# The opening of a two-layer block on one core: more warming products, sums of squares on another engine, and a product moved

## The chip, the cores and the metric

The kernel runs on one core of a Trainium2 chip. The metric is device time in microseconds (us), from one launch. A core has TensorE (PE in the profile; PEld is its weight loading), VectorE (DVE), ScalarE (ACT), GpSimd (POOL) and SyncE (SP), which here only issues transfers. Each works through its own instructions in order; semaphores tie them together.

## The reference, cut to what matters

A two-layer block and a third mixing block are applied to 256 tokens of width 1024, in float32. Only the start of the first layer is touched by the change:

```
h  = rmsnorm(x, a_norm_attn)                # x * rsqrt(mean(x*x) + eps) * gain
z  = h @ a_w_in                             # q, k (768 each), v (768), qm (256)
q, k = rope(q), rope(k)
o_self = diff_attention(q, k, v)            # 6 heads of 2 x 64
kv = rmsnorm(mem, a_mem_norm) @ a_w_mem_kv  # memory keys, values (256 each)
o_mem  = softmax(qm @ mk / 8) @ mv          # 4 heads
x  = x + concat(o_self, o_mem) @ a_w_out
```

After it come an MLP, a second layer of the same kind with its MLP, and the mixing block with a gated MLP.

## The kernel before, in words

Activations lie transposed, 8 chunks of 128 features by 256 tokens. To keep float32 accuracy each operand is split: `hi` is a rounded copy (written by ScalarE, L206, L191, L270, L276), `lo` is the rest (VectorE, L216, L192, L271, L280), and a product is three matmuls, hi x hi, hi x lo and lo x hi.

The product work is a list of **units**. A unit is one weight tile (512 KB) and 24 matmuls of 256 columns. In the opening: units 0 to 5 are the values `v` (three `tok_block`s, PSUM name `tp`), units 6 and 7 the memory queries `qm` (`fp`), units 8 to 11 the memory keys and values from `hMa` (two of `fp`, two of `tp`), units 12 and 13 the first query-key block (`fp`), and so on through six query-key blocks. Norms are applied late: the products use x times the gain, and the row factor rsqrt(mean) comes in when PSUM is read. So the sum of squares `ssq_A` is needed by two small products, `mst` (L374's input, per token) and `ms` (L348's input, per column), whose results become `rstdt_A`, `rstd_A` and then the scaled rope tables `ropeR` (L905, POOL).

`Stat.add` (L302 to L308) forms that sum: ScalarE squares a chunk into `sq` (four buffers), and an addition onto `acc` follows, seven for eight chunks, on POOL.

The order of all else is set by a planner at build time. `Order.t` is a model clock that advances with the matmuls alone, 106.7 ns for one of 256 columns (a float32 one of 256 columns counts 427 ns). Side jobs are generators: `yield 450` means to go on at the first poll after 450 ns of model time, and polls come between matmuls, after 4, 10, 12, 16, 22 and 24 of a `tok_block` unit and after each 4 of a `feat_block` unit. At a poll, due side jobs are written first and then at most one piece of weight preparation (`hi` of a tile, then the two halves of `lo`) for a tile about 2.25 to 4 units ahead. So each engine has a fixed order, and a position in it can be given as the number of matmuls issued before it ("position 88"). In the first layer a weight transfer is issued by SP when a tile's second `lo` half is done (four `raw` buffers).

`first_inputs` (from L929) issues the first transfers, puts 10 warming products of `ones` on TensorE (L939), which write a tile nobody reads, and splits the first chunks. `squares()` starts the eight additions with 450 ns between them and then `tok_stat` and `row_stat` with a delay of 3500. `memory_a()` splits the memory into `hMa` chunk by chunk (hi, 600, lo, 500) and sums its squares (`ssq_M`) from model time 9200. `lambdas()` puts small operations on VectorE from 15000 (identb, maskb, lscr). `mem_pair` is the attention of two memory heads; the first is spawned after the first query-key block and the second after the second. `head_a` is the attention of one self head, spawned 6500 after its query-key block; it begins with the scores `S`, which need `q` and `k` from the rope (VectorE L623, L624, then POOL L625, L626).

PSUM tiles `acc` have four buffers, taken in turn: each block takes the two that the block before last has given back.

Of the kernel before, what the change touches and what calls it, by code (L numbers as in the profile page):

```python
# [13 lines left out]
OP = mybir.AluOpType  # L14
# [94 lines left out]
def block_kernel(ctx: ExitStack, tc: tile.TileContext, a, out):  # L109
    nc = tc.nc  # L110
# [10 lines left out]
    O = Order()  # L121
    E = SimpleNamespace()
# [10 lines left out]
    def ps_tile(name):  # L133
        return psB.tile([P, 512], F32, tag="ps", name=name)

    def w_tile(name, shape=(P, S), bufs=2):
        return phase[1].tile(list(shape), F32, tag=name, name=name, bufs=bufs)
# [4 lines left out]
    def s_tile(name, n, bufs=4):  # L142
        return small.tile([P, n], F32, tag=name, name=name, bufs=bufs)
# [26 lines left out]
    def hook(fn):  # L170
        plan.append((len(wlist), 0, fn))
# [117 lines left out]


    class Stat:
        def __init__(self, name):
            self.acc = big.tile([P, S], F32, tag="ssq", name="ssq_" + name, bufs=2)
            self.first = None
            self.n = 0

        def add(self, src, keep=False):
            if keep:
                sq = w_tile("sqk", bufs=KC)
            else:  # L300
                sq = wk.tile([P, S], F32, tag="sq", name="sq", bufs=4)
            nc.scalar.activation(sq, src, AF.Square)  # L302
            if self.n == 0:
                self.first = sq
            elif self.n == 1:
                nc.gpsimd.tensor_tensor(self.acc, self.first, sq, OP.add)
            else:
                nc.gpsimd.tensor_tensor(self.acc, self.acc, sq, OP.add)  # L308
            self.n += 1
            return sq  # L310

# [40 lines left out]
    def rstd_tile(name):  # L352
        return big.tile([P, S], F32, tag="rstd", name="rstd_" + name, bufs=3)

    def row_stat(st, name, then=None, delay=1000, tile_fn=None, table=None):
        yield delay
        yield from O.take("rs")
        y = rstd_tile(name)
        v, src = yield from ms_row(st.acc, D, tile_fn=tile_fn)
        yield from rsqrt_(y, v, then=table, src=src)  # L360
        O.give("rs")
        setattr(E, "r" + name, y)
        if then:
            then()
        O.mark("r" + name)

    def tok_stat(st, name, delay=1000):
        yield delay
        yield from O.take("ps")
        p = ps_tile("mst")  # L370
        for j in range(2):
            mm(p[:, 2 * j:2 * j + 2], st.acc[:, j * P:(j + 1) * P], ones[:, 0:2], start=True, stop=True)
        v = s_tile("msvt", 4)
        nc.vector.tensor_scalar(v, p[:, 0:4], 1.0 / D, EPS, OP.mult, OP.add)  # L374
        y = big.tile([P, 4], F32, tag="rstdt", name="rstdt_" + name, bufs=3)
        yield from rsqrt_(y, v, src=(p[:, 0:4], 1.0 / D, epsc[:, 0:1], 1))
        setattr(E, "t" + name, y)
        O.mark("t" + name)
# [392 lines left out]
    PAUSE_MA = (1500, 0, 1100, 2000, 600, 2200)  # L771
# [65 lines left out]
    def mem_kv(src, h, kv):  # L837
        def evac_k(n, p):
            O.need("rM")
            if n == 0:  # L840
                pool = phase[1] if kv == "ma" else big
                setattr(E, kv + "k", pool.tile([P, 2, S], F32, tag="mk", name=kv + "k", bufs=1))
                setattr(E, kv + "v", pool.tile([P, 2, S], F32, tag="mv", name=kv + "v", bufs=1))
            nc.vector.tensor_tensor(getattr(E, kv + "k")[:, n, :], p, E.rM, OP.mult)
            if n == 1:
                O.mark(kv + "k")
        feat_block(src[0], lambda: (h(), h()), evac_k)
        put_v = scaled_tok(lambda: getattr(E, kv + "v"), 0, "tM")

        def evac_v(j, p):  # L850
            put_v(j, p)
            if j == 1:
                O.mark(kv + "v")
        tok_block(src[1], 256, h, evac_v)
# [73 lines left out]
    def first_inputs():  # L928
        nc.scalar.dma_start(par[:, 0:C_LAM], a["par"][:, 0:C_LAM])  # L929
        for i in range(4):  # L930
            nc.sync.dma_start(xT[:, 2 * i:2 * i + 2, :], a["xT"][:, 2 * i:2 * i + 2, :])
            w_load((slice(2 * (i % 2), 2 * (i % 2) + 2),), i % 2)
        w_load()
        w_load()
        E.hA = operand("hA")
        stA = Stat("A")
        warm = ps_tile("warm")
        for _ in range(10):
            nc.tensor.matmul(warm[:, 0:P], ones, ones, start=True, stop=True)  # L939
        for k in range(KC):  # L940
            split_scaled(E.hA, k, xT[:, k, :], gain(G_A_ATTN, k))
            if k % 2:
                w_split(k // 4, slice(k % 4 - 1, k % 4 + 1))
        w_piece()
        w_piece()
        w_piece()

        def tables():
            E.tr = rope_tables(E.rope_a, E.rA)

        def squares():
            for k in range(KC):
                stA.add(xT[:, k, :])
                yield 450
            O.spawn(tok_stat(stA, "A", 3500))
            O.spawn(row_stat(stA, "A", tables, 3500))

        def second_inputs():
            nc.sync.dma_start(memT, a["memT"])
            yield 8100  # L960
            nc.sync.dma_start(E.rope_a, a["rope_a"])
            nc.sync.dma_start(par[:, C_LAM:C_END], a["par"][:, C_LAM:C_END])
            nc.sync.dma_start(cst, a["cst"])

        O.spawn(squares())
        O.spawn(second_inputs())
        E.v = p_tile("vA", (P, 2, 768))
        E.o = operand("oA")
        O.spawn(lambdas(), 15000)
        O.spawn(bias_rows(), 40000)  # L970
        O.spawn(memory_a(), 9200)
        O.spawn(memory_b())

    def lambdas():
# [24 lines left out]
    def memory_a():  # L999
        E.hMa = operand("hMa")  # L1000
        stM = Stat("M")
        yield from split_chunks(E.hMa, memT, G_A_MEM, 500, stM)
        O.spawn(row_stat(stM, "M", None, 3000))
        O.spawn(tok_stat(stM, "M", 3000))
        O.mark("hMa")
# [8 lines left out]
    def wait_for(key, fn):  # L1014
        def get():
            O.need(key)
            return fn()
        return get
# [4 lines left out]
        tok_block(a["w_a_v"][i], 256, lambda: E.hA, scaled_tok(lambda: E.v, 256 * i, "tA"),  # L1023
                  acc_tile if i else ps_tile, "tA")
    mem_queries(a["w_a_qm"], lambda: E.hA, "rA")
    mem_kv(a["w_a_mem"], wait_for("hMa", lambda: E.hMa), "ma")
    for h in range(6):
        qk_block(a["w_a_qk"][h], lambda: (E.hA, E.hA), wait_for("rA", lambda: E.tr),
                 lambda q, k, h=h: head_a(h, q, k), 6500)
        if h in (0, 1):  # L1030
            hook(lambda h=h: O.spawn(mem_pair(h, "ma", 6 + h, "oA", PAUSE_MA)))
    mem_kv(a["w_b_mem"], wait_for("hMb", lambda: E.hMb), "mb")

    def staged(first, stat, g, last, name, also=None):
# [572 lines left out]
```

## Time and profile before

| what | value |
|---|---|
| median of 3 runs | 943.23 us (942.23 to 943.95) |
| profiled execution | 943.52 us, of which the span is 941.7 us |
| busy share | PE 97%, PEld 91%, DVE 73%, ACT 58%, POOL 21% |
| mean granted TensorE clock | 0.993 of full speed |
| share of the chain that ended last | PE 80%, DVE 8%, ACT 5%, POOL 3%, DMA 2% |

The span runs from the first instruction to the last; 1.8 us lie around it. The page also shows the span in 40 slices of 23.5 us; the change lies in the first five. A row of the timeline gives start, duration, engine, line, operation, output and inputs, and in brackets how long the engine was idle before it and who ended that.

### The profile page before, as it was taken

What the parts mean: (1) busy time and instruction counts of PE and PEld (TensorE: products, weight loads), DVE (VectorE), ACT (ScalarE), POOL (GpSimd) and SP (SyncE); (2) the same over time, 40 slices, a digit from 0 to 9 for tenths busy, and PEclk for the clock granted to TensorE, in tenths of its full rate; (3) what the DMA queues carried; (4) which work ended last, traced back from release to release, by engine and by line L of the source; (5) the groups of instructions that cost most, each with busy time, mean ns of one, the idle gap of its engine ahead of it and who ended that gap; (6) DMA issues with size and microseconds to landing.
All of it is one profiled execution on the core that took longest, in us unless ns stands there. A gap on an engine that the chain in (4) does not pass through costs nothing.

```text
span 941.7 us, 17731 instructions
## 1 busy us (share of the span) xinstructions
PE 916.3 (97%) x6768; PEld 855.2 (91%) x6768; DVE 688.9 (73%) x1434; ACT 549.5 (58%) x1063; POOL 199.4 (21%) x238
## 2 busy tenths in 40 slices
PE   7899999999999999999999999999898999999998
PEld 7898899999999998899999999999877989999998
DVE  6979978776666598876776666687956788766664
ACT  6747666665555574656665555566475666545551
POOL 3415633000000042322000000055656421001010
PEclk9899999999999999999999999999999999999999
DMA  8653444565555535333575555574413456665551
GB/s 288 200 178 112 149 145 127 193 229 191 195 185 192 187 119 197 107 118 94 189 255 180 179 187 193 188 259 144 134 67 114 155 172 194 217 200 169 195 199 46
DMA packets 45686, 161.10 MB, mean 171 GB/s; under 512 B 5128, under 2 KB 6800, under 8 KB 45216
## 3 DMA queue, kind: packets, MB, share of 16 engines
q1 hardware_dynamic: 45104, 158.14, 51.3%
q0 software_dynamic: 208, 1.63, 0.6%
q8 instruction: 53, 0.87, 0.4%
q14 instruction: 33, 0.27, 0.1%
q10 hardware_dynamic: 288, 0.18, 0.1%
HBM read 158.88 MB, written 2.63 MB: 172 GB/s over the span
## 4 chain that ended last, share of the span: by engine, by line
PE 80%; DVE 8%; ACT 5%; POOL 3%; DMA 2%; issue 2%; DVEq 0%; SPq 0%; POOLq 0%; ACTq 0%
PE fp L149 40%; PE acc L149 32%; DVE lo L216 2%; PE tp L149 2%; ACT hi L206 2%; PE S L149 1%; DMA raw<-in_w_a_v_dram 1%; POOL rsh L625 1%; PE O L149 1%; PE Sm L149 1%; PE T L154 1%; PE ms L149 1%; DVE xT L603 1%; DVE nm L678 1%; POOL ssq_A L308 1%
## 5 line engine op out<-in xcount | busy, mean ns | idle before, releaser
L216 DVE TENSOR_TENSOR lo<-raw,hi 128x512 fp32r<-128x512 f32 (+1 forms) x555 | 381.5, 733 | 134.9 <-ACT hi L206 134.4
L206 ACT ACTIVATE hi<-raw 128x1024 fp32r<-128x1024 f32 x287 | 296.2, 1053 | 124.9 <-PE acc L149 47.8
L149 PE MATMUL acc<-u,hi 128*128 128x256 f32 x1376 | 245.0, 281 | 0.0
L149 PEld LDWEIGHTS acc<-u,hi 128*128 128x128 f32 x1376 | 210.5, 188 | 0.0
L149 PE MATMUL acc<-u,lo 128*128 128x256 f32 x688 | 193.0, 281 | 0.0
L149 PEld LDWEIGHTS acc<-u,lo 128*128 128x128 f32 x688 | 129.9, 189 | 0.0
L149 PE MATMUL fp<-hW,hi 128*128 128x512 f32 (+1 forms) x368 | 96.2, 384 | 0.1
L450 ACT ACTIVATE uc<-fp 128x256 f32<-128x256 f32 x108 | 39.4, 379 | 63.6 <-PE fp L149 63.6
L149 PE MATMUL fp<-hV,hi 128*128 128x512 f32 (+1 forms) x272 | 70.1, 381 | 0.0
L149 PE MATMUL fp<-hU,hi 128*128 128x512 f32 (+1 forms) x272 | 70.0, 381 | 0.0
L149 PEld LDWEIGHTS fp<-hW,hi 128*128 128x128 f32 x368 | 61.4, 188 | 7.6 <-DVE uc L453 0.3
L453 DVE TENSOR_TENSOR uc<-fp,uc 128x256 f32<-128x256 f32 x108 | 43.8, 418 | 28.5 <-ACT uc L450 27.7
L149 PEld LDWEIGHTS fp<-hW,lo 128*128 128x128 f32 x352 | 53.6, 188 | 7.2
L149 PE MATMUL fp<-hW,lo 128*128 128x256 f32 x352 | 55.9, 281 | 0.0
L149 PEld LDWEIGHTS fp<-hV,hi 128*128 128x128 f32 x272 | 45.2, 189 | 5.2
L149 PEld LDWEIGHTS fp<-hU,hi 128*128 128x128 f32 x272 | 45.2, 188 | 5.2
L875 ACT ACTIVATE uu<-uc 128x256 f32<-128x256 f32 x64 | 24.1, 418 | 39.2 <-DVE uc L871 39.2
L890 POOL TENSOR_TENSOR uc<-uc,rstd_W 128x256 f32<-128x256 f32 x22 | 15.9, 743 | 146.0 <-ACT uc L888 146.0
L149 PE MATMUL fp<-hZ,hi 128*128 128x256 f32 x304 | 45.1, 287 | 0.0
L149 PEld LDWEIGHTS fp<-hV,lo 128*128 128x128 f32 x256 | 38.9, 188 | 5.3
L149 PEld LDWEIGHTS fp<-hU,lo 128*128 128x128 f32 x256 | 38.9, 188 | 5.2
L598 DVE TENSOR_TENSOR u<-uu,u 128x256 fp32r<-128x256 f32 x64 | 24.3, 422 | 25.4 <-ACT u L596 25.4
(345 smaller groups left out, 1634.0 us busy)
## 6 DMA issues: line engine op xcount, KB each, us to landing
raw<-in_w_a_up_dram SPq DMA_DIRECT2D x32, 512.0 KB, 4.7
raw<-in_w_a_down_dram SPq DMA_DIRECT2D x32, 512.0 KB, 4.5
raw<-in_w_b_up_dram SPq DMA_DIRECT2D x32, 512.0 KB, 4.6
raw<-in_w_b_down_dram SPq DMA_DIRECT2D x32, 512.0 KB, 4.7
raw<-in_w_gate_dram SPq DMA_DIRECT2D x22, 512.0 KB, 4.5
raw<-in_w_up_dram SPq DMA_DIRECT2D x22, 512.0 KB, 4.7
raw<-in_w_down_dram SPq DMA_DIRECT2D x22, 512.0 KB, 4.5
raw<-in_w_a_qk_dram SPq DMA_DIRECT2D x12, 512.0 KB, 4.3
```

The lines of the kernel that those rows point to most:

```text
L149: nc.tensor.matmul(dst, lhsT, rhs, **kw)
L154: nc.tensor.transpose(dst, src, ident)
L206: nc.scalar.activation(hi, raw, AF.Copy)
L216: eng.tensor_tensor(lo[sl], raw[sl], f32v(hi[sl]), OP.subtract)
L308: nc.gpsimd.tensor_tensor(self.acc, self.acc, sq, OP.add)
L450: nc.scalar.activation(c, p[:, S:2 * S], AF.Copy)
L453: nc.vector.tensor_tensor(c, p[:, 0:S], c, OP.add)
L598: nc.vector.tensor_tensor(u[:, 1, n, :], us[n], f32v(u[:, 0, n, :]), OP.subtract)
L603: nc.vector.tensor_tensor(x, bank, x, OP.add)
L625: nc.gpsimd.tensor_tensor(sh, sh, sinr, OP.mult)
L875: nc.scalar.activation(u, t, AF.Square)
L890: nc.gpsimd.tensor_tensor(g, g, rs, OP.mult)
```

## The change

Three things, all in the first layer's opening:

1. 15 warming products on TensorE in place of 10.
2. The seven additions of `ssq_A` go to VectorE (`ssq_M` and all later sums stay on POOL). The delay of the two small products behind them is 4500 in place of 3500, and `memory_a()` starts at model time 12000 in place of 9200.
3. The memory product (`mem_kv`, four units) is put behind the first query-key block: units 8 and 9 are now query-key block 0, units 10 to 13 the memory product. The two memory attentions are spawned after query-key blocks 1 and 2 in place of 0 and 1.

```diff
     class Stat:
-        def __init__(self, name):
+        def __init__(self, name, engine=None):
+            self.engine = engine or nc.gpsimd
...
             elif self.n == 1:
-                nc.gpsimd.tensor_tensor(self.acc, self.first, sq, OP.add)
+                self.engine.tensor_tensor(self.acc, self.first, sq, OP.add)
             else:
-                nc.gpsimd.tensor_tensor(self.acc, self.acc, sq, OP.add)
+                self.engine.tensor_tensor(self.acc, self.acc, sq, OP.add)
...
-        stA = Stat("A")
+        stA = Stat("A", nc.vector)
         warm = ps_tile("warm")
-        for _ in range(10):
+        for _ in range(15):
             nc.tensor.matmul(warm[:, 0:P], ones, ones, start=True, stop=True)
...
-            O.spawn(tok_stat(stA, "A", 3500))
-            O.spawn(row_stat(stA, "A", tables, 3500))
+            O.spawn(tok_stat(stA, "A", 4500))
+            O.spawn(row_stat(stA, "A", tables, 4500))
...
-        O.spawn(memory_a(), 9200)
+        O.spawn(memory_a(), 12000)
...
-    mem_kv(a["w_a_mem"], wait_for("hMa", lambda: E.hMa), "ma")
     for h in range(6):
         qk_block(a["w_a_qk"][h], lambda: (E.hA, E.hA), wait_for("rA", lambda: E.tr),
                  lambda q, k, h=h: head_a(h, q, k), 6500)
-        if h in (0, 1):
-            hook(lambda h=h: O.spawn(mem_pair(h, "ma", 6 + h, "oA", PAUSE_MA)))
+        if h == 0:
+            mem_kv(a["w_a_mem"], wait_for("hMa", lambda: E.hMa), "ma")
+        if h in (1, 2):
+            hook(lambda h=h: O.spawn(mem_pair(h - 1, "ma", 5 + h, "oA", PAUSE_MA)))
     mem_kv(a["w_b_mem"], wait_for("hMb", lambda: E.hMb), "mb")
```

## Rows read from the trace of the kernel before

**Rows 1.** The page's busy time of each engine, share of the span, instructions.
```profile
PE 916.3 (97%) x6768; PEld 855.2 (91%) x6768; DVE 688.9 (73%) x1434; ACT 549.5 (58%) x1063; POOL 199.4 (21%) x238
```

**Rows 2.** The waits of PE, whole span: us in total, times, longest.
```profile
PE mst L149 <- POOL ssq_A L308: 2.8, 1, 2.8
PE fp L149 <- DVE hMa L280: 2.7, 2, 2.2
...
PE ms L149 <- ACT osq L751: 2.1, 2, 1.1
```

**Rows 3.** Timeline of PE, units 0 to 4: start, duration, instruction, idle before.
```profile
1.06 3.84 PE L939 MATMUL warm<-ones 128*128 128x128 f32 x20 [1.06 <-DVE ones L254]
7.04 1.02 PE L149 MATMUL tp<-hi,hA 128*128 128x256 f32 x4 [2.15 <-ACT hi L191]
...
11.56 0.64 PE L149 MATMUL tp<-hi,hA 128*128 128x256 f32 x4
...
14.44 0.64 PE L149 MATMUL tp<-hi,hA 128*128 128x256 f32 x4
...
18.70 0.63 PE L149 MATMUL tp<-hi,hA 128*128 128x256 f32 x4
22.11 0.61 PE L149 MATMUL mst<-ones,ssq_A 128*128 128x2 f32 x4 [2.77 <-POOL ssq_A L308]
...
24.04 0.64 PE L149 MATMUL tp<-hi,hA 128*128 128x256 f32 x4
```

**Rows 4.** Timeline of PE, units 8 to 14, memory product and first query-key block.
```profile
35.35 1.11 PE L149 MATMUL fp<-hMa,hi 128*128 128x256 f32 x8
...
42.14 0.58 PE L149 MATMUL fp<-hMa,hi 128*128 128x256 f32 x1 [2.17 <-DVE hMa L280]
...
59.21 1.12 PE L149 MATMUL fp<-hA,hi 128*128 128x256 f32 x8
```

**Rows 5.** Stretches: PE, PEld, DVE, ACT, POOL busy, granted clock, DMA share, GB/s.
```profile
9.00:10.00 1.00, 1.00 (x6) 1.00 (x6) 1.00 (x4) 1.00 (x3) 0.00 (x0) 0.50 1.04 342
...
21.00:22.00 1.00, 0.00 (x0) 0.00 (x0) 1.00 (x2) 0.00 (x0) 1.00 (x1) 1.00 1.01 401
...
46.00:47.00 1.00, 1.00 (x6) 1.00 (x6) 0.96 (x4) 0.87 (x3) 0.00 (x0) 0.50 0.89 283
```

**Rows 6.** Timeline of ACT: the third tile's hi and the last square.
```profile
12.55 1.06 ACT L206 ACTIVATE hi<-raw 128x1024 fp32r<-128x1024 f32 x1 [1.41 <-DMA raw<-in_w_a_v_dram]
...
17.66 0.40 ACT L302 ACTIVATE sq<-xT 128x256 f32<-128x256 f32 x1
```

**Rows 7.** Timeline of DVE: lo halves, statistics, last hMa, first rope.
```profile
15.82 6.78 DVE L216 TENSOR_TENSOR lo<-raw,hi 128x512 fp32r<-128x512 f32 x6 [0.88 <-ACT hi L206]
22.75 0.16 DVE L374 TENSOR_SCALAR msvt<-mst 128x4 f32<-128x4 f32 x1
...
25.71 0.42 DVE L337 TENSOR_TENSOR rs256t<-rs256y 128x256 f32<-128x256 f32 x1
...
41.61 0.47 DVE L280 SCALAR_TENSOR_TENSOR hMa<-memT,par,hMa 128x256 fp32r<-128x256 f32 x1
...
58.48 0.41 DVE L623 TENSOR_TENSOR rt<-fp,ropeR 128x256 f32<-128x256 f32 x1
```

**Rows 8.** Timeline of POOL: sum for x, rope tables, first rope.
```profile
15.61 6.44 POOL L308 TENSOR_TENSOR ssq_A<-ssq_A,sq 128x256 f32<-128x256 f32 x6
...
30.32 3.75 POOL L905 TENSOR_TENSOR ropeR<-rope_a,rstd_A 128x256 f32<-128x256 f32 x4 [2.28 <-DVE hMa L280]
...
61.85 1.05 POOL L626 TENSOR_TENSOR k<-rt,rsh 128x256 f32<-128x256 f32 x1
```

**Rows 9.** DVE by line, 42.1 to 53.6 us, POOL idle: busy, mean ns.
```profile
L216 DVE TENSOR_TENSOR lo<-raw,hi 128x512 fp32r<-128x512 f32 x10 | 6.4, 681 | 1.4 <-ACT hi L206 1.4
```

**Rows 10.** Busy time in longer stretches (columns as in Rows 5).
```profile
22.10:42.10 20.00, 17.34 (x141) 16.88 (x141) 18.34 (x37) 14.95 (x33) 11.19 (x14) 0.98 0.62 204
...
59.20:85.00 25.80, 24.98 (x185) 21.50 (x183) 23.63 (x60) 16.97 (x51) 11.21 (x13) 1.00 0.37 120
```

## The prediction

> **What bounds the kernel now.** I read the page's busy line first: TensorE is busy for 916.3 of 941.7 us [rows 1], so time can come only from stretches where it stands or runs at a low clock. Then PE's waits: of those 25.4 us of idleness 2.8 are for the sum of squares on POOL and 2.7 for the memory's low parts [rows 2], both in the opening. PE's timeline puts them in place. The warming products end at 4.90, PE stands 2.15 us, and unit 0 then takes 4.52 us (7.04 to 11.56) where unit 1 takes 2.88 (11.56 to 14.44) [rows 3]. The stretches tell why: the clock is at 0.50, its 1.2 GHz level, in 9 to 10 us [rows 5]. From 19.33 to 22.11 PE stands for `ssq_A` [rows 3]. In units 8 to 13 it waits twice for low parts of `hMa`, 2.7 us in all [rows 2], the second time for 2.17 [rows 4], and behind that the clock is at 0.50 again, as in 46 to 47 us [rows 5].
>
> The second reading is of DVE. While POOL adds squares, six low halves take 6.78 us, 1.13 each [rows 7]; with POOL idle ten take 6.4, 0.64 each [rows 9]. From 22.1 to 42.1 DVE is busy for 18.34 of 20 us [rows 10]: it runs that stretch, and PE catches up with it at 42.1. That decides the second half of the change.
>
> **The change part by part.** The sum is made against the profiled execution, 943.5 us (941.7 of span and 1.8 around it), 0.3 above the median of the runs.
>
> *Five more warming products.* Twenty records of ten products take 3.84 us, so five more take 1.9 and end at 6.8, still before the first real product at 7.04 [rows 3]. They delay nothing; PE's gap shrinks from 2.15 to about 0.2 us, and unit 0 should run at full clock, 1.6 us shorter. Little of that arrives: unit 2 needs the high part of the third tile, whose transfer ends at 12.55 and whose copy ends at 13.61 [rows 6], against 14.44 now [rows 3]. So the gain is at most 0.83; its first low half then takes 0.64 [rows 9] to about 14.3, 0.2 us after unit 2 would ask for it. Bounds 0 and 0.85; I take 0.7.
>
> *Sums on VectorE.* The trace has no addition of two SBUF tiles of 128x256 on DVE there, but a multiplication of that shape takes 0.42 us and starts 0.45 before its successor [rows 7]. Seven cost 2.9 to 3.2 us (with POOL in the way they could cost 0.9 each, nearer to its own 1.07 [rows 8], but POOL then has nothing to do). Against that, six low halves lose their company: 6 x (1.13 - 0.64) = 2.9 us. DVE is even. In its order four additions stand ahead of the fourth tile's first low half, the last two behind its second half. With squares of 0.40 us as now, the last at 17.66 [rows 6], I get DVE at 14.9, four additions to 16.7, low half to 17.3, addition, low half to 18.3, two additions to 19.2. The sum is ready at 19.2, not 22.06 (POOL's end [rows 8]).
>
> *The delay of 4500.* Today the two small products stand at position 88: PE has issued 14 groups of six and four more when it stops [rows 3]. One thousand model ns are 9.4 matmuls; the next poll puts them at position 96, the end of unit 3. PE gets there at 16.7 + 2.9 = 19.65, after 19.2. The wait of 2.77 goes. Bounds: 2.3 (sum half a microsecond late) and 2.8; I take 2.8. Unit 4 starts at about 20.5 in place of 24.04. SP's queue loses nothing: its weight transfers follow low halves that end at or before today's times, and the rope tables' transfer stands at the same place in its order.
>
> *Memory product behind the first query-key block.* Today 35.35 to 59.21 [rows 4] holds six units and the memory's own statistics: 6 x 2.88 + 0.8 = 18.1 us of 23.9. The excess, 5.8, is 2.7 of waits and 3.1 of half clock. Now the positions. `memory_a` moves from 9200 to 12000, so its last low part from position 188 to 220 (eight chunks, 16 matmuls apart in the later units); its first use, chunk 7 in the second memory unit, moves from 224 to 272. That is 16 matmuls or 1.9 us more slack. But PE comes 3.5 us earlier and DVE does not: it stands at the statistics at about 22.4, after the low halves queued there, against 22.75 now. From there to the last low part of `hMa` it needs today's 19.3 us (22.75 to 42.08 [rows 7]), plus three more low halves (1.9 [rows 9]) and the two `qm` operations (0.7, each like the rope's first [rows 7]), which the new order puts ahead, less some 1.0 of today's 1.66 us of idleness [rows 10]. That is 43.3. PE asks for it at 20.5 + (272 - 96)/24 x 2.88 + 0.8 = 42.4: a wait of 0.9.
>
> What is late next: the values' units (12 and 13) take the PSUM buffers of query-key block 0, which DVE must have read in its rope, placed at position 240 behind three further low halves: it begins at 45.2 and frees the first buffer at 46.0. PE would be at unit 12 at 45.2; 0.8 more. Then head 0's scores, which stand at about position 300 (spawned 6500 after block 0). Behind them on PE everything queues. The rope takes 4.4 us from DVE's first operation to `k` (58.48 to 62.90 [rows 7, 8]), so `k` is ready at about 49.5, and PE reaches the scores at 47.4: 2.1. Together 3.8 us of waits in place of 5.8, each under the length at which the clock fell: gain 2.0. Bounds: nothing gained if DVE is 2 us later than this, and 5.8 if its company with POOL (rope tables 3.75 us [rows 8] and memory sums) costs less than today.
>
> The granted clock kept 1.00 over the wait of 2.77 us, as in 21 to 22 us, and fell to 0.50 over those of 2.15 and 2.17 [rows 3, 4, 5]. The Trainium skill ("TensorE: Matmul & The Clock Gate", What's actually happening) says why one cannot count on either: the activity window runs freely, so the point of change differs from run to run. By that rule the three new waits, too, may cost a fall of 3.1 us in some runs; the trace agrees in that a longer gap was harmless and shorter ones were not.
>
> *Attention spread anew.* Head 0 comes four units earlier and memory pairs 0 and 1 two units later; heads 1 to 5 keep their positions. The largest of today's waits there is 2.1 us in two parts, for head 0's and another head's squares on ACT [rows 2], while DVE is busy 23.6 of 25.8 us from 59.2 to 85.0 [rows 10]. It starts this stretch some 5 us behind PE and has 2.2 of slack in it to catch up, so I add 0.6 us of waits, between the two bounds: -1, if head 0's early start takes half of those waits away, and +3, if the part of the 5 us that the slack doesn't cover is met as waits.
>
> Sum: -0.7 - 2.8 - 2.0 + 0.6 = -4.9, so 943.5 - 4.9 = 938.6. What follows the first layer's output product is untouched, and PE is busy there nearly throughout, so the gain should pass to the end.
>
> **The rivals.**
>
> *DVE does not hold the memory units back.* If low halves beside the rope tables run at 0.64 and the waits of 3.8 us vanish, the gain is 0.7 + 2.8 + 5.8 = 9.3: about 934.5. For it: sums for x no longer hinder DVE. Against: DVE's 18.34 us busy of 20 without slack.
>
> *The clock falls in the new waits.* The second half's gain becomes 2.0 - 3.1 = -1.1 and the total -0.7 - 2.8 + 1.1 + 0.6 = -1.8: 941.7, about the line where no change can be told (0.2% or 1.9 us is what a measurement of this kernel can tell). For it: a gap of 2.1 us stands before the scores. Against: PE works right up to it.
>
> *The sum is late after all.* If squares or additions slip behind the low halves, PE stands for 2 us at position 96 as it did at 88; total -2.9: 940.6.
>
> *Slower: DVE becomes the bound of the opening.* All the low halves between positions 96 and 240 (15) at 1.13 in place of 0.64, with the three or so already counted as slow left out, would put DVE's rope of block 0 some 6 us later. PE then stands 6 us at head 0's scores, the clock falls (3.1), and against the 4.9 gained this gives +4.2: 947.7. It decides from about 5 us of added DVE delay. For it: the first low halves beside POOL did run at 1.13. Against: POOL has only 14 operations in 22 to 42 us [rows 10], and seven fewer before.
>
> **How the numbers follow.** The forecast's own case (936.5 to 940.9) 0.54 with the late sum in it; waits gone (933.5 to 936.5) 0.16; falling clock 0.20 (940.9 to 943.5), half of it within 0.2%; slower 0.06; a change that its own later waits eat up, no difference, 0.04. Faster by over 0.2%: 0.54 + 0.16 + 0.10 = 0.80; within: 0.10 + 0.04 = 0.14; slower: 0.06. The range is 934.2 to 942.4; it leaves out some of the best case and of the worst, 0.2 together.
>
> **What would show it.** Warming ends near 6.8 and the clock stays at 1.00 in 7 to 11 us; unit 2 starts near 13.7. No wait before `mst`; unit 4 near 20.5; low halves at about 0.65 in 16 to 22 us. The first query-key block at about 31.8 without a long wait; waits of PE for `hMa`, for the rope's buffers or for `k` of about 1 to 2 us each between 41 and 50. The prediction is wrong if `mst` still waits over 1 us, if the clock is at 0.50 anywhere in 40 to 55, or if waits in 55 to 120 exceed 6 us.

## The result, and the profile after

The changed kernel takes 947.99 us (median of 5 runs, 946.69 to 948.97). Its time relative to the kernel before is 1.0058, 95% interval 1.0044 to 1.0072: slower by 0.58%, where the prediction named 0.2% as what a measurement of this kernel can tell. The forecast was 938.6, and 947.99 lies outside its range. The profiled execution took 947.97 us, 4.45 more than that of before. Of the 947.97 us 2.3 lie around the span, in place of 1.8.

The page's first lines of after:

```profile
span 945.7 us, 17749 instructions
...
PE 918.9 (97%) x6778; PEld 856.8 (91%) x6778; DVE 686.4 (73%) x1441; ACT 549.4 (58%) x1063; POOL 191.0 (20%) x231
```

Against [rows 1] PE is busy 2.6 us longer for 10 records more, while DVE and POOL are busy for less. PE's timeline of after shows where the time goes (start, duration, instruction, idle before):

```profile
1.05 6.19 PE L940 MATMUL warm<-ones 128*128 128x128 f32 x30 [1.05 <-DVE ones L254]
7.00 0.72 PE L149 MATMUL tp<-hi,hA 128*128 128x256 f32 x4
...
13.50 0.74 PE L149 MATMUL tp<-hi,hA 128*128 128x256 f32 x4 [0.20 <-ACT hi L206]
...
19.80 0.50 PE L149 MATMUL mst<-ones,ssq_A 128*128 128x2 f32 x4
...
20.50 0.82 PE L149 MATMUL tp<-hi,hA 128*128 128x256 f32 x4
...
42.63 1.19 PE L149 MATMUL fp<-hMa,hi 128*128 128x256 f32 x8 [3.36 <-DVE qm L862]
...
57.69 1.12 PE L149 MATMUL fp<-hA,hi 128*128 128x256 f32 x8
...
87.42 0.55 PE L154 MATMUL T<-cst,dw 128*128 128x128 f32 x3 [2.04 <-DVE brow L922]
...
120.86 0.70 PE L149 MATMUL ms<-osq,ones 128*128 128x256 f32 x2 [2.27 <-ACT osq L752]
131.66 0.39 PE L149 MATMUL acc<-oA,hi 128*128 128x256 f32 x2
```

Four marks cut the opening into pieces that can be set against before: unit 4 (20.50, before 24.04), unit 14 (57.69, before 59.21 [rows 4]), the first layer's output product `acc<-oA` (131.66, before 127.49) and the end of the span.

| piece | before | after | difference at equal work | forecast |
|---|---|---|---|---|
| start to unit 4 | 24.04 | 20.50 | -3.5 | -3.5 |
| unit 4 to unit 14 | 35.17 | 37.19 | +0.9 | -2.0 |
| unit 14 to `acc<-oA` | 68.28 | 73.97 | +6.3 | +0.6 |
| `acc<-oA` to the end, and around the span | | | +0.8 | 0 |

("At equal work": head 0's scores, 1.1 us on PE, now lie ahead of unit 14; they are taken from the second piece and added to the third. One pair of `ms` products, 0.5 us, lies ahead of `acc<-oA` in after and behind it in before; it is taken from the third piece and added to the last. The last has 0.45 us around the span in it.)

The clock and the busy time of DVE, in stretches of after (columns as in [rows 5]):

```profile
7.00:11.00 4.00, 4.00 (x36) 3.98 (x35) 3.96 (x9) 3.76 (x9) 0.00 (x0) 1.00 0.99 339
...
26.00:46.00 20.00, 15.71 (x122) 15.13 (x121) 19.40 (x36) 14.75 (x30) 10.91 (x14) 0.95 0.58 205
44.00:47.00 3.00, 3.00 (x15) 2.82 (x14) 3.00 (x8) 1.06 (x1) 0.00 (x0) 0.51 0.67 201
59.20:85.00 25.80, 24.00 (x184) 20.89 (x182) 19.48 (x49) 16.45 (x41) 10.15 (x12) 1.00 0.42 132
88.00:92.00 4.00, 4.00 (x16) 3.25 (x16) 2.55 (x9) 3.83 (x14) 0.71 (x2) 0.57 0.08 17
122.00:126.00 4.00, 4.00 (x24) 3.67 (x24) 2.75 (x9) 1.83 (x3) 2.46 (x4) 0.57 0.38 136
```

The clock now stays at 1.00 in 7 to 11 us. In 26 to 46 DVE is busy for 19.40 of 20 us: it is the engine that runs there, and PE stands. In 59.2 to 85, where before has DVE busy for 23.63 us [rows 10], after has 19.48: DVE has more idle time there, so it isn't short of capacity. Behind the waits at 42.63, 87.42 and 120.86 the clock falls.

PE's waits from 57 to 135 us (total, times, longest), first in before, where the largest of the three stands in [rows 2] (2.1 us; 3.9 in all), then in after:

```profile
PE S L149 <- POOL k L626: 1.0, 1, 1.0
PE OA L149 <- ACT wT L698: 0.8, 1, 0.8
```

```profile
PE ms L149 <- ACT osq L752: 2.3, 1, 2.3
PE T L154 <- DVE brow L922: 2.0, 1, 2.0
PE Tm L154 <- ACT rs256l L320: 1.3, 1, 1.3
PE Tm L154 <- ACT wTm L814: 0.6, 1, 0.6
PE pbias L149 <- DVE on L758: 0.5, 1, 0.5
PE T L154 <- ACT wTm L814: 0.2, 1, 0.2
```

After's six are 6.9 us, 3.0 more than before. The two falls of the clock (88 to 92 and 122 to 126 us, granted 0.57 in each stretch) cost 2 x 4 x 0.43 = 3.4 more. Together that is the piece's 6.3, within 0.1.

DVE's timeline of after, first the sums, then the end of the memory split and the rope, then the place where PE waits for `brow`:

```profile
14.69 0.42 DVE L307 TENSOR_TENSOR ssq_A<-sq 128x256 f32<-128x256 f32 x1
15.21 1.48 DVE L309 TENSOR_TENSOR ssq_A<-ssq_A,sq 128x256 f32<-128x256 f32 x3
...
18.15 0.95 DVE L309 TENSOR_TENSOR ssq_A<-ssq_A,sq 128x256 f32<-128x256 f32 x2
19.02 3.10 DVE L216 TENSOR_TENSOR lo<-raw,hi 128x512 fp32r<-128x512 f32 x5
22.03 0.16 DVE L375 TENSOR_SCALAR msvt<-mst 128x4 f32<-128x4 f32 x1
...
42.07 0.74 DVE L862 SCALAR_TENSOR_TENSOR qm<-fp,rstd_A 128x256 f32<-128x256 f32 x2
...
44.34 0.47 DVE L280 SCALAR_TENSOR_TENSOR hMa<-memT,par,hMa 128x256 fp32r<-128x256 f32 x1
...
46.54 0.41 DVE L624 TENSOR_TENSOR rt<-fp,ropeR 128x256 f32<-128x256 f32 x1
...
84.04 0.48 DVE L758 SCALAR_TENSOR_TENSOR on<-OA,subg,ors 128x256 f32<-128x256 f32 x1 [1.11 <-POOL ors L334]
...
86.83 0.54 DVE L922 COPY brow<-pbias 8x384 f32<-8x384 f32 x1
```

The sums end at about 19.1, low halves without POOL beside them go at 0.62 us (five in 3.10) where [rows 7] has 1.13. But `msvt` begins at 22.03, only 0.7 us earlier than in before, and the last low part of `hMa` ends at 44.81 where before has 42.08 [rows 7] (by the prediction's positions the changed order puts three low halves and `qm` ahead of it). PE gained 3.5 us up to unit 4; DVE gained 0.7.

### The profile page after: what moved, and what is told of

Same layout as the page of the kernel before. It is cut to its first block, busy times and chain, and to the rows that moved or that the text cites. A ratio compares the mean times of both kernels' runs of the same rounds, so it can differ in the third digit from the quotient of the medians.

```text
span 945.7 us, 17749 instructions
## 1 busy us (share of the span) xinstructions
PE 918.9 (97%) x6778; PEld 856.8 (91%) x6778; DVE 686.4 (73%) x1441; ACT 549.4 (58%) x1063; POOL 191.0 (20%) x231
## 4 chain that ended last, share of the span: by engine, by line
PE 78%; DVE 9%; ACT 5%; DMA 3%; issue 3%; POOL 2%; DVEq 0%; SPq 0%; ACTq 0%; POOLq 0%
PE fp L149 39%; PE acc L149 32%; DVE lo L216 3%; ACT hi L206 2%; PE tp L149 2%; PE S L149 1%; DMA raw<-in_w_a_v_dram 1%; POOL rsh L626 1%; PE T L154 1%; PE O L149 1%; DMA raw<-in_w_a_qm_dram 1%; PE ms L149 1%; PE Sm L149 1%; DVE xT L604 1%; DVE hZ L616 1%
## 5 line engine op out<-in xcount | busy, mean ns | idle before, releaser
L216 DVE TENSOR_TENSOR lo<-raw,hi 128x512 fp32r<-128x512 f32 (+1 forms) x555 | 377.2, 726 | 139.9 <-ACT hi L206 139.4
L149 PEld LDWEIGHTS fp<-hW,lo 128*128 128x128 f32 x352 | 53.6, 188 | 7.2
```

Of the source, the lines that this page charges most:

```text
L149: nc.tensor.matmul(dst, lhsT, rhs, **kw)
L216: eng.tensor_tensor(lo[sl], raw[sl], f32v(hi[sl]), OP.subtract)
```

## The experiments

Theory after the first look: the loss comes from the move behind query-key block 0, by what it does to the positions of side jobs in 57 to 130 us. Rival: DVE, which the sums load, is late in the opening, and all the rest follows from that. Ratios are against the kernel before, run beside each kernel; line numbers in the diffs are left out.

### The two halves by themselves

Opening alone, the kernel before with the first two parts, but `memory_a()` still at 9200:

```diff
+        stA = Stat("A", nc.vector)
...
+        for _ in range(15):           # warming
...
+            O.spawn(tok_stat(stA, "A", 4500))
+            O.spawn(row_stat(stA, "A", tables, 4500))
```

> The kernel before with 15 warming products, the sum of squares on VectorE and the delay of 4500; the memory product stays in front of query-key block 0 and the memory split starts at 9200 as before. Theory (the opening is sound, the loss comes from the new order of the memory product): PE reaches unit 4 at about 20.5 us as in the changed kernel, 3.5 us ahead of the kernel before, and the time is 2 to 4 us below the kernel before (939 to 941), because the wait for the memory's low parts may grow by what PE is ahead. Rival (the seven additions put VectorE so far behind that the attention stretch pays for it): no gain or slower, 943 to 948, with waits of over 6 us between 58 and 132 us as in the changed kernel.

Move alone, the kernel before with the third part and `memory_a()` at 12000:

```diff
+        if h == 0:
+            mem_kv(a["w_a_mem"], wait_for("hMa", lambda: E.hMa), "ma")
+        if h in (1, 2):
+            hook(lambda h=h: O.spawn(mem_pair(h - 1, "ma", 5 + h, "oA", PAUSE_MA)))
...
+        O.spawn(memory_a(), 12000)
```

> The kernel before with only the memory product put behind query-key block 0, its two attentions a block later and the memory split from 12000; 10 warming products, sums on GpSimd, delay 3500. Theory (the move costs the time): 946 to 951, 3 to 8 us above the kernel before, with waits of 6 us or more and a low clock between 58 and 132 us. Rival (VectorE's additions are to blame): 940 to 944, not above the kernel before.

The opening alone: 943.53 us, ratio 1.0023 [1.0012, 1.0033]. The move alone: 946.19, 1.0056 [1.0044, 1.0068], with the waits of after in 57 to 135 us (ms 2.2, `brow` 2.0, Tm 1.7 and 0.6, pbias 0.5), and 73.65 us from unit 14 to `acc<-oA`. In the opening alone that piece takes 68.3, as in before. So the third piece's loss belongs to the move. But the opening's gain of 3.5 us didn't arrive either: its time is the rival's, above before, though without the waits that the rival named for it. PE's timeline and a stretch of the opening alone:

```profile
33.56 1.10 PE L149 MATMUL fp<-hMa,hi 128*128 128x256 f32 x8
...
39.50 0.50 PE L149 MATMUL fp<-hMa,hi 128*128 128x256 f32 x2 [1.36 <-DVE hMa L280]
42.10 0.58 PE L149 MATMUL fp<-hMa,hi 128*128 128x256 f32 x1 [2.10 <-DVE hMa L280]
...
47.30 0.64 PE L149 MATMUL tp<-hi,hMa 128*128 128x256 f32 x4
```

PE reaches the memory product 1.8 us earlier than before (33.56 against 35.35 [rows 4]), waits 4.2 us for `hMa` in three parts, runs at half clock from 40 to 47 us, and leaves for the transposed units at 47.30 where before left at 47.64.

### What in the move loses

After, with the bias rows at 100000 in place of 40000:

```diff
-        O.spawn(bias_rows(), 40000)
+        O.spawn(bias_rows(), 100000)
```

> The changed kernel, but the small job that makes the bias rows (one product, one copy on VectorE, three small transfers) starts at model time 100000 in place of 40000, so it lies in the MLP. Theory A (this job takes a PSUM buffer in front of a head's transposition while VectorE is behind: waits of 0.5 and 2.0 us and then about 3.7 us at half clock, 1.9 lost): 4 us less than the changed kernel, about 944. Theory B (the job is only where the delay shows; without it the same chain of VectorE, ScalarE and GpSimd stops PE elsewhere): within 1.5 us of the changed kernel, 946.5 to 948.

After, with the memory attentions where before has them (behind blocks 0 and 1):

```diff
-        if h in (1, 2):
-            hook(lambda h=h: O.spawn(mem_pair(h - 1, "ma", 5 + h, "oA", PAUSE_MA)))
+        if h in (0, 1):
+            hook(lambda h=h: O.spawn(mem_pair(h, "ma", 6 + h, "oA", PAUSE_MA)))
```

> The changed kernel, but the two memory attentions are spawned right behind the memory product and behind query-key block 1 (in the changed kernel: behind blocks 1 and 2), so they stand at the positions that they had in the kernel before. Theory (their later place piles them on heads 1 to 3): 3 to 6 us less than the changed kernel, 942 to 945. Rival (their place does not matter, the delay is carried over from the opening): within 1.5 us of the changed kernel.

Both together:

> The changed kernel with both corrections of the attention stretch: memory attentions a block earlier and the bias rows at model time 100000. Theory (each of the two places side work where VectorE, ScalarE and GpSimd wait on one another in a ring, and the losses are separate): about 5 us below the changed kernel, within 2 us of the kernel before, with at most 4 us of waits between 58 and 132 us. Rival (one chain stops PE whatever stands in it): like the earlier pairs alone, 3.5 us or more above the kernel before.

Measured: bias rows later 946.21, 1.0049 [1.0034, 1.0064]; attentions early 945.15, 1.0040 [1.0028, 1.0052]; both 943.96, 1.0021 [1.0012, 1.0030]. The first two gave less than the 4 and the 3 us or more that were expected. These kernels move `pbias` (0.8 us on PE), and a head's `OA` and `ms`, behind `acc<-oA`, so the third piece can't be compared by that mark. From unit 14 to the second layer's first product, which holds all of them, the traces have (lines of before, after, both together; unit 14 of both together is at 58.91):

```profile
332.41 0.63 PE L149 MATMUL tp<-hi,hK 128*128 128x256 f32 x4
336.15 0.63 PE L149 MATMUL tp<-hi,hK 128*128 128x256 f32 x4
332.92 0.63 PE L149 MATMUL tp<-hi,hK 128*128 128x256 f32 x4
```

That is 272.1 us in before (less head 0's scores), 278.5 in after, 276.1 with the bias rows later, 275.3 with the attentions early, 274.0 with both. With the bias rows moved, the waits for `brow` and at `pbias` are gone; with both, the waits of PE from 57 to 135 us are

```profile
PE ms L149 <- ACT e L684: 1.7, 1, 1.7
PE ms L149 <- DVE on L758: 1.6, 1, 1.6
PE T L154 <- ACT rs256l L320: 1.5, 1, 1.5
PE Sm L149 <- DVE oA L287: 1.5, 1, 1.5
```

6.3 us, hardly less than after's 6.9, where at most 4 were expected; but no fall of the clock lies behind them in this trace. Each alone overlaps after in its interval, both together don't. So the two placements account for most of the third piece's loss, 4.5 of 6.4 us by this mark, and with them put right the move is worth nothing: 1.0021 with it, 1.0023 without. What they take away is mostly the clock's share, 3.4 of the 4.5. With both together it shows over all timed executions too: their mean granted clock is 0.992 and 0.989 in the two sets of after, 0.991 in the move alone, 0.992 with either placement alone (not clearly higher) and 0.995 with both, as in before (0.994 to 0.995). Why waits of nearly the same sum are followed by fewer falls isn't shown. How `brow` makes PE wait can be followed through three engines that each work in order: POOL has head 0's norm (`ors`) behind a rope and is done with it at 84.0; DVE stands 1.11 us for it at `on` (84.04); behind `on` and 2.3 us of other work lies `brow` (86.83), which empties the PSUM tile that `pbias` wrote; and PE, at 85.4, needs a tile for `T`.

### Moving DVE's own work

The opening alone with `lambdas` at 25000 in place of 15000, and the corrected move with it at 24000:

```diff
-        O.spawn(lambdas(), 15000)
+        O.spawn(lambdas(), 25000)
```

> The opening alone (15 warming products, sums on VectorE, delay 4500, memory product in its old place), with the small VectorE operations of lambdas() (identb, maskb, lscr, nlam) started at model time 25000 in place of 15000, behind the memory's last low part. Theory (VectorE's order decides when the last low part of the memory comes, so whatever PE gains in the opening it waits for there): those operations take 3.4 us between 31 and 35 us, so the wait for hMa falls from 4.2 to about 1 us, no fall of the clock follows, and the time is 3 to 6 us below the opening alone and 1 to 4 below the kernel before. Rival (the low parts come late because of ScalarE or a transfer): the wait stays above 3 us and the time within 1.5 us of the opening alone.

> The same as the one with pairs and bias moved, and lambdas() at 24000 in place of 15000, which takes 3.4 us of VectorE's time from in front of the qm read and the memory's low parts. Theory (VectorE is the bound of 26 to 48 us): the wait of 3.4 us at the memory product (PSUM buffers of qm, read by VectorE at 42.1) becomes under 0.5, the clock does not fall behind it, and the time is 3 to 6 us below the kernel without this. It would then be below the kernel before by 2 to 5 us. Rival: the wait moves to the rope of block 0 or to head 0's scores and the gain is under 1.5 us.

The opening alone with `lambdas` later: 942.35, 1.0007 [0.9999, 1.0016]; the wait for `hMa` is 2.9 in place of 4.2, the last `hMa` ends at 40.4 in place of 42.05. That is 1.2 us by the medians (0.4 of it around the span), though the intervals overlap: the low parts do come earlier when DVE has less ahead of them, but a gain in time isn't settled, and the 3 to 6 us that were expected are not there. The corrected move with it: 943.88, 1.0021 [1.0008, 1.0033], nothing gained, as its rival had it; unit 14 begins 2.3 us earlier (56.59 against 58.91) and `acc<-oA` only 0.4 earlier (125.97 against 126.39): what arrives early there waits later, and the clock falls once more (78 to 82 us).

The other buffer: after, with the `qm` products in the PSUM buffers of the values, so that the memory product doesn't wait for them:

```diff
-    mem_queries(a["w_a_qm"], lambda: E.hA, "rA")
+    mem_queries(a["w_a_qm"], lambda: E.hA, "rA", ps_tile)
```

> The changed kernel, but the two memory-query products use PSUM buffers of the other set, so that the memory product need not wait for VectorE to have read them. Theory (that buffer is what the wait of 3.4 us is for): the wait named after qm is gone; the next late thing is the last low part of the memory (VectorE at 44.8), so PE starts the memory product at about 39.5 and waits some 2 us in it; the total of waits there falls by 1 to 2 us and the time by 0 to 3 us. Rival (the wait is really for weights or hMa, only named after qm): the wait stays at 3 us under another name at the same place.

> The changed kernel, unchanged, timed and profiled again beside the others. Expected as before: 0.4 to 0.7% above the kernel before, with the waits of 3.4 us for the qm buffers and of about 7 us between 58 and 132 us. If the falls of the clock at 88 and at 122 us are a matter of the execution, one of them is missing or lies elsewhere, while the waits agree to 0.2 us.

After again: 947.99, 1.0062 [1.0044, 1.0081], with the same waits. The falls behind 57 us lie elsewhere in its trace: one long one from 87.5 to 94.5 us behind the wait for `brow`, none at 122, together again 3.4 us lost. With the other buffers: 948.01, 1.0064 [1.0047, 1.0081]; the expected fall of the waits by 1 to 2 us didn't come. The wait of 3.4 us is gone, and these waits of PE up to 57 us stand in its place:

```profile
PE S L149 <- POOL k L627: 2.4, 1, 2.4
PE fp L149 <- DVE lo L216: 1.4, 3, 0.7
...
PE fp L149 <- DVE hMa L280: 0.5, 1, 0.5
```

Together again 4.3 us, as in after (3.4 for `qm`, 0.5 for `vA`, 0.4 for a low half), now most of it at the scores of head 0, where the prediction had set 2.1. The low clock has moved along, from 44 to 47 to 52 to 55 us, and unit 14 starts at 59.22, no earlier than in after. So the buffer decided where PE did its waiting, and not how long; that DVE sets the pace of this stretch is the reading that fits (here DVE is busy for 19.49 of 20 us in 30 to 50).

The memory's split without its pauses, in the opening alone and in the kernel before:

```diff
-        O.spawn(lambdas(), 15000)
+        O.spawn(lambdas(), 25000)
-        yield from split_chunks(E.hMa, memT, G_A_MEM, 500, stM)
-        O.spawn(row_stat(stM, "M", None, 3000))
-        O.spawn(tok_stat(stM, "M", 3000))
+        yield from split_chunks(E.hMa, memT, G_A_MEM, 0, stM)
+        O.spawn(row_stat(stM, "M", None, 9000))
+        O.spawn(tok_stat(stM, "M", 9000))
```

> The opening alone (memory product in its old place) with lambdas() at 25000 and the memory split without its pause of 500 between chunks, so that its last low part stands some 30 to 44 matmuls earlier in VectorE's order; the memory's statistics keep their place (delay 9000). Theory (in the opening alone the gain of PE is turned into the wait for hMa, and that wait brings the fall of the clock, 3.2 us): no wait above 0.7 us and no low clock between 30 and 50 us, PE at the second memory block's tp products at about 40.5 in place of 46 to 47, and a time 4 to 7 us below the opening alone, 2 to 5 below the kernel before. Rival (another input of the memory product is as late, the low half of its weights or ssq_M): a wait of 2 us or more stays there, gain under 2 us.

> The kernel before with the same two edits of the memory split and lambdas(), but with 10 warming products, sums on GpSimd and delay 3500. Theory: the wait of 2.7 us and the fall behind it go, 2 to 5 us below the kernel before; the wait of 2.8 us for ssq_A stays, so it is 1 to 3 us above the opening with the same edits. Rival (the opening's edits gain nothing whatever follows): equal to the opening with the same edits within 1 us.

Both are below before: 940.08, 0.9976 [0.9964, 0.9988], and 941.14, 0.9984 [0.9975, 0.9994], the second by less than 0.2% and less than was expected. The first has the lowest median here. In both the waits for `hMa` are gone, since its last low part ends at 37.6 and 36.8 us. In the first a new one stands in their place, which its expectation had ruled out, from its timeline of PE:

```profile
30.49 2.08 PE L149 MATMUL fp<-hA,hi 128*128 128x256 f32 x8 [3.39 <-ACT vA L834]
```

ACT had stood 4.55 us for the transfer of the memory, with the statistics of x queued behind that, and the clock is at 0.51 in 29 to 36 us. The two intervals overlap, so whether the opening's parts are worth anything once the memory is fast isn't settled.

### Warming and sums each alone, and before again

The opening's loss of 0.23% was still open: PE has one stall less, and one fall less than in the first trace of before. Two kernels split it, and the kernel before was traced three times more.

> The kernel before, unchanged, profiled a second time, as a yardstick for what differs from one execution to the next. If the clock falls of the first profile (7 to 11 us and 41 to 48 us) belong to the kernel, they stand here too, and the row of waits is the same; if they are a matter of the execution, at least one of them is missing and the time is up to 3 us less (940 to 941). Waits of PE should agree to 0.2 us in either case.

Warming alone and the sums with their delay alone, each on the kernel before:

```diff
+        for _ in range(15):           # warming alone
...
+        stA = Stat("A", nc.vector)    # sums alone
+            O.spawn(tok_stat(stA, "A", 4500))
+            O.spawn(row_stat(stA, "A", tables, 4500))
```

> The kernel before with 15 warming products and nothing else. Theory A (the sums on VectorE are what loses, by standing in DVE's order ahead of the memory's low parts): the clock stays at 1.00 in 7 to 11 us, mst then waits some 3.4 to 3.6 us for POOL in place of 2.8 to 3.2, everything from unit 4 on stands as before; 941.0 to 942.0, ratio 0.9995 to 1.0005. Rival B (the earlier start itself loses, because a fall saved at 9 us comes back at the longer wait for mst or at hMa): ratio 1.001 to 1.0025.

> The kernel before with the sums of squares on VectorE and the delay of 4500, 10 warming products. Theory A: mst does not wait, PE reaches the memory product about 1 us earlier than before, waits 3.5 to 4.2 us for hMa in 34 to 47 us and falls to half clock there; 943.0 to 943.7, ratio 1.0015 to 1.0025, the time around the span 2.2 us as in the opening alone. Rival B: it is no slower than before, 941.0 to 942.0. Rival C (neither part alone loses; only both together bring PE so early that hMa is waited for three times): both of these two kernels within 0.1% of before, hMa wait here 2.5 to 3.5 us.

> The kernel before a third time, for a trace of one of its usual executions (its timed ones lie at 941.4, the two profiled ones at 943.5 and 944.8). If a fall of the clock makes the difference: span 939 to 940.5, the same waits for ssq_A (2.8 to 3.2) and hMa (2.0 to 2.7), and at most one fall before 60 us. Rival: fewer waits for hMa (below 1.5 us) with the falls where they were.

> As the third: a second chance for a usual execution, span 939 to 940.5; the out product of the first layer would then start at about 125.5 in place of 127.5 and 128.8.

Before again was timed at 941.62, 1.0004 [0.9994, 1.0013]; its three new traces are of executions of 944.81, 943.77 and 942.50 us. Warming alone: 942.61, 0.9999 [0.9990, 1.0007]. Sums and delay alone: 944.19, 1.0021 [1.0011, 1.0030]. So the sums and their delay lose it (which of the two, no run separates), and warming does nothing. Neither of the last two traces of before came to the span of 939 to 940.5 us that was hoped for (942.0 and 940.7). The traces (start of `mst`, of the memory product, waits for `hMa`, end of its last low part, start of the transposed memory units; us):

| trace | `mst` | memory product | waits | `hMa` done | transposed |
|---|---|---|---|---|---|
| before, as in the rows | 22.11 | 35.35 | 2.7 | 42.08 | 47.64 |
| before again | 22.43 | 37.24 | 2.0 | 43.03 | 48.54 |
| before, third | 22.28 | 37.10 | 2.0 | 42.85 | 47.49 |
| before, fourth | 22.79 | 39.04 | 0.6 | 43.42 | 46.48 |
| warming alone | 22.94 | 39.16 | 0.4 | 43.30 | 46.35 |
| sums alone | 20.21 | 33.91 | 3.6 | 41.82 | 46.47 |
| opening alone | 20.63 | 33.56 | 4.2 | 42.05 | 47.30 |

Two of them in stretches of PE (PE busy, granted clock, DMA share, GB/s), first the fourth of before, then the sums alone:

```profile
22.00:29.00 7.00, 6.21 (x27) 0.55 0.90 293
...
40.00:47.00 7.00, 6.40 (x53) 1.00 0.56 173
```

```profile
22.00:29.00 7.00, 5.71 (x49) 1.00 0.82 295
...
40.00:47.00 7.00, 5.12 (x28) 0.76 0.60 210
```

In its fourth trace before loses its time early: the clock falls behind the wait for `mst`, PE is at the memory product 3.7 us later than in the rows, finds `hMa` nearly done and leaves at 46.48. The sums alone save all that, arrive 5.1 us earlier, wait, fall later, and leave at 46.47. `hMa` is done between 41.8 and 43.4 in all of them. What PE saves ahead of the memory product it spends there, on DVE. The other traces of before leave later than the sums alone, at 47.5 to 48.5.

That shows how a gain at `mst` can be gone 25 us later. Why the sums alone are 0.2% slower, their own trace doesn't place. Over all executions timed in that sitting their mean granted clock is no lower (0.9953 against 0.9946); 0.45 us lies around the span (2.23 against 1.77) and 1.3 in it, but the profiled execution was among the shortest (span 939.9, the median is 942.0) and doesn't show it. The opening alone, which loses as much, was profiled at its own median (943.53), and the fourth trace of before at that kernel's (942.50 against 942.48). Set side by side, the opening alone leaves the memory units 0.8 us later (47.30 against 46.48) and begins the second layer 0.8 later (331.93 against 331.16); with the 0.45 around the span that is about half of its 0.23%, by one trace of each, from two sittings. The rest stays open.

## Why the prediction was wrong

**The step that failed** is "*Attention spread anew*", "so I add 0.6 us of waits, between the two bounds": +0.6 with -1 and +3 for ends, and +6.3 measured. The 0.6 itself was worked out from no row. The step priced the heads' order by the slack of DVE, and DVE was not short of time there (19.48 us busy in 59.2 to 85, less than before). The move alone shows this loss, and the two placements take away 4.5 us of it. What it had left out: moving four units changes which small jobs stand ahead of which on each in-order engine, though many of them (`bias_rows` among these) keep their own position; and PSUM tiles taken by such a job (`pbias`) make PE wait for an engine that has nothing to do with PE's next product. Some 3.4 of the 6.3 is the clock behind the new waits, for which the sum had nothing; its rivals priced one for the memory units and one at head 0's scores.

**Steps that came as forecast**: warming ends at 7.24 (6.8), no low clock in 7 to 11 us, unit 2 at 13.50 (13.7), `mst` at 19.80 without a wait (19.65), unit 4 at 20.50 (20.5), low halves at 0.62 (about 0.65). The last `hMa` came at 44.81, 1.5 us behind the 43.3. The -3.5 read from these was right at unit 4 and wrong at the end: the opening alone is 0.23% slower than before. "The wait of 2.77 goes ... I take 2.8" took a wait for a cost in a stretch where the prediction itself had read that DVE "runs that stretch, and PE catches up with it". The term was sized from one trace, in which no fall lay behind the wait for `mst`; in the three others of before the wait is 3.2 and the clock falls behind it, and the one with the longest of these falls is the shortest of the four (942.50 us). Time lost there need not be time lost at the end.

The term for warming, 0.7, was sized from the low clock in 7 to 11 us, and there luck came in. The three other traces of before, with 10 warming products, have none there:

```profile
7.00:11.00 4.00, 4.00 (x30) 3.63 (x31) 3.92 (x9) 3.74 (x8) 0.00 (x0) 1.00 0.99 329
7.00:11.00 4.00, 4.00 (x30) 3.60 (x30) 3.90 (x9) 3.60 (x8) 0.00 (x0) 1.00 1.03 377
7.00:11.00 4.00, 4.00 (x28) 3.27 (x26) 3.44 (x8) 3.40 (x8) 0.00 (x0) 1.00 1.00 374
```

Of the seven traces with 10 warming products here two have that fall (the first of before, and the sums alone at 8 to 12 us), of the eleven with 15 none. So the fall belonged to the execution that was read. More warming may make it rarer, but by the runs warming alone gains nothing (0.9999).

**Memory product**, "3.8 us of waits in place of 5.8 ... gain 2.0": measured +0.9. The 5.8 were 2.7 of waits and 3.1 of low clock, and the 3.8 had no low clock in them. The waits before 57 us were 4.3, near to the 3.8, but in one piece of 3.36 at the memory product, on the buffers of `qm`, where three shorter ones had been set at `hMa`, the rope and the scores. I had asked for the next user of query-key block 0's buffers and not of the `qm` units' two, one block earlier. When that was taken away the waits came at the scores, with unit 14 no earlier. Behind the 3.36 the clock fell (0.51 in 44 to 47), which cost 1.7 us. The reason given for leaving that out, that each new wait was shorter than those behind which the clock fell, failed with the waits' lengths, and the prediction's own row of a harmless 2.77 us spoke against a fixed length.

**The rivals.** The falling clock came true in its mechanism, not in its size: it was given 941.7. (The rival of gone waits comes to 934.2 by its own terms and not to 934.5, which changes nothing.) The slower one had the time, 947.7, and not the place: PE doesn't stand 6 us at head 0's scores, and most of the loss lies after 57 us. Of the three conditions that the prediction named for being wrong one holds, the clock at 0.50 in 40 to 55. The waits in 55 to 120 come to about 6.0 (6.9 in 57 to 135, less 0.9 of the last one), at the limit of 6, which was set too wide to warn: the falls behind them weren't in it.

## What to carry to other kernels

Before counting a removed wait as a gain, find the engine that sets the next 20 us: here, with the memory product in its old place, DVE finished the memory's split at 42 to 43 us whatever PE had saved, and the only edits that paid were those that let DVE finish it sooner (0.24%, and 0.16%, which is hard to tell). When a block of products moves, list each side job by what now stands ahead of it on every in-order engine, and by whose PSUM tile it takes; here a copy of 8 rows and two attentions one block later cost 0.4% between them, most of it through the clock. A single trace of a kernel may show one of several ways to lose the same microseconds: with two or three traces, terms that only trade places show as such.

## What the hardware did that was not expected

*The clock moves between executions of one program.* In four traces of the same kernel before, the wait for `mst` was once 2.77, and the clock kept 1.00, and three times 3.2, and it was at 0.50 behind that, in 23 to 26 us in two traces and in 23 to 29 in one. In 7 to 11 us it was low in one of the four. Behind waits for `hMa` of 2.17 and twice 2.0 it fell, behind 0.6 it did not. The Trainium skill ("TensorE: Matmul & The Clock Gate", What's actually happening) says that the window is free-running and the point of change varies from run to run; these traces agree: the same wait was followed by low stretches of different length. What one low stretch took from PE was about 1.7 us or twice that, as the first 170 us of all traces here add up (0.57 over 4 us in 88 to 92 of after; 0.51 over 7 us in 29 to 36 of the opening alone with the fast memory).

*Where it falls matters.* The third and the fourth trace of before each lost 3.4 us to the clock up to 60 us. The third lost half of it ahead of the memory product and half behind, and left the memory units at 47.49; the fourth lost all of it ahead, waited 0.6 us for `hMa` in place of 2.0, and left at 46.48. It is the shortest of the four. One pair of traces shows this: time lost ahead of a wait that DVE ends was in part time that PE would have waited.

*Time around the span.* It is 1.8 us in before and in eight other kernels, and 2.2 to 2.3 in five: after (both times), the bias rows later, the other buffers, the opening alone and the sums alone. Delaying `lambdas` in the opening alone, or putting the attentions back in after, brings it back to 1.8 or 1.9. It is 0.45 us of the 4.8 that after lost, and nothing in the traces explains it.
